# A hybrid decoder block on one core: the end of a gathered tile, its weights, the one-hots of the gates and the layout of the gates

## The chip, the cores and the metric

The kernel runs on one core of a Trainium2 chip. The metric is the time of one execution in device microseconds; the kernel before takes 4811.26 us, the median of three runs from 4801.93 to 4822.15. TensorE multiplies matrices, VectorE, ScalarE and GpSimd work element by element, SyncE only issues transfers, and ScalarE and GpSimd issue transfers too. In the profile they are PE (PEld for the load of its weights), DVE, ACT, POOL and SP; SPq and ACTq are their queues.

## What is computed

A decoder block over 1024 tokens of width 1024: differential attention and a Mamba-2 mixer in parallel, merged, projected and normalised, then a layer of experts (PEER). The change touches only this last layer. Every token picks 8 x 16 = 128 of 16384 experts by its routing scores, and each expert is one row of u and one of v:

```python
top_s, pos = lax.top_k(cand_s, PEER_TOPK)
eidx = jnp.take_along_axis(cand_i, pos, axis=-1)
g = jax.nn.softmax(top_s, axis=-1)
act = jax.nn.gelu(jnp.einsum('thkd,td->thk', expert_u[eidx], tb), approximate=False)
wts = (g * act.astype(jnp.float32)).astype(tb.dtype)
return jnp.einsum('thk,thkd->td', wts, expert_v[eidx])
```

The result, scaled by a gate, is added to 1.19 times the residual x1, and a layer norm (ln2) follows.

## The kernel before

The tokens lie in two halves of four tiles of 128. `run()` (line 1447) first drives the main phase, which is everything up to the routing scores of both halves, and then the dense phase, in the pool `dp`. Each of the two is a generator whose steps have costs. `drive()` emits a step of it and gives the work beside it as much credit as that step cost; `step()` spends the credit on two queues, "side" (gathered tiles) and "urgent" (routing). A scheduler then sets each engine's order by priority, with the main or dense work and everything in `inline()` ahead; each engine runs its own instructions in that order, and GpSimd's is the order of emission. When the dense work is all emitted, what is left of the side work follows.

The experts are worked in two ways.

**Gathered tiles** are tiles 0 and 1 of the first half and 6, 5 and 4 of the second, in this order. `gathered()` (line 1115) loads the tile's hidden rows into gh. Then for each of 128 choices k an indirect transfer on GpSimd (line 1182) brings one row of u for every token into a buffer grow, and VectorE multiplies it with gh and sums it up into act (line 1125). After the gelu, act is transposed into wt. Then 128 transfers bring the rows of v, each for one token, with a row for each of its 128 experts, and TensorE multiplies them with that token's column of weights (line 1290, ps_y). For this the column stands between columns of zeros in a tile own, so that token r's result falls on row r of a group of 16 (OWN) and adds zero to the others. VectorE copies the columns into two own tiles in turn, 2 tokens for each of two halves at a time (line 1152), 32 copies for a tile. The results go through ys into y_d in DRAM. The tile's end follows at once: gy is read back (line 1176), `finish()` (line 1189) loads x1 and three rows of parameters (gr) and does five passes and some small operations on VectorE, and the result is stored. SyncE issues these loads, the next tile's gh and the dense weights in one queue.

**Dense tiles** are 2, 3 and 7: all 16384 experts are computed for them, and the unpicked ones get a gate of zero. `spread()` (line 1228), part of the routing, makes the gates. For each token k a one-hot first_k, scaled by the gates, is made on VectorE (line 1256) and a one-hot second_k on GpSimd (line 1259), 128x128 each, and their product on TensorE (ps_gate) is that token's gate for each of 128x128 experts. Four tokens are copied into a quarter of gs on ScalarE (line 1273), and after eight the single gs buffer is stored into g_d on ScalarE's queue (line 1277). Tiles 2 and 3 are spread during the main phase but for tile 3's last tokens; tile 7 is spread when the dense phase has begun.

`dense()` (line 1292) goes through 128 blocks of 128 experts. Block e's u weights (wraw, split in two parts whi and wlo by ScalarE and VectorE) give ps_u and act_t. Some blocks later, for f = e - lead, act_t is multiplied with the gates gl (line 1322), split into ehi and elo, and multiplied with the weights of v into ps_v. gl holds the gates of eight blocks for three tiles; it is loaded with three transfers when f % 8 == 0 (line 1319), into one of two buffers:

```python
gt = dp.tile([P, len(tiles) * 16, 8, 8], F32, name="gl", tag="gl", bufs=2)
for i, t in enumerate(tiles):
    nc.sync.dma_start(gt[:, i * 16 : i * 16 + 16], self.g_d[t][:, :, f : f + 8, :])
```

g_d is laid out as [expert row, group of 8 tokens, block, token in the group], so a store writes 4 KB in a run and a load reads 8 x 8 numbers, 256 bytes, in a run. Before the first f, `await_gates()` emits routing until tiles 2, 3 and 7 are spread.

Of the kernel before, what the change touches and what calls it, by code (L numbers as in the profile page):

```python
# [47 lines left out]
class Block:  # L48
# [25 lines left out]
    def setup(self):  # L74
# [39 lines left out]

        self.own = []
        for i in range(2):
            self.own.append(cp.tile([P, 4, 31 + OWN], F32, name=f"own{i}"))
            nc.gpsimd.memset(self.own[i], 0.0)

# [14 lines left out]
        self.g_d = {  # L134
            hb * 4 + t: dr.tile([P, 16, P, 8], F32, name=f"g_d{hb * 4 + t}")
            for hb in range(2) for t in range(self.few[hb], 4)
# [977 lines left out]


    def gathered(self, tile_no):
        nc, a, gp = self.nc, self.a, self.gp
# [5 lines left out]
        for k in range(NSEL):  # L1123
            u = self.gather(a["peer_u"], ei, k)
            nc.vector.scalar_tensor_tensor(  # L1125
                u, u, 1.0, h2, op0=ALU.mult, op1=ALU.mult, accum_out=act[:, k : k + 1]
            )
            yield 1.2
        nc.scalar.activation(act, act, AF.Gelu)
# [7 lines left out]

        n = 2 * OWN
        rows = deque()
        for k in range(P + self.rows_by):  # L1140
# [3 lines left out]
            if k >= self.rows_by and k % 2:  # L1144
                j = k - self.rows_by
                b, r = j // n, j % n // 2
                if r == 0:
                    yield from self.claim("side")
                    ps = self.psum("ps_y", tag="gate")
                own = self.own[r // 2 % 2]  # L1150
                if r % 2 == 0:
                    nc.vector.tensor_copy(  # L1152
                        own[:, :, OWN - 1].rearrange("p (h r) -> p h r", h=2),
                        wt[:, b * n : b * n + n].rearrange("p (h r) -> p h r", h=2)[:, :, r : r + 2],
                    )
                for half in range(2):
                    v = rows.popleft()
                    left = own[:, half * 2 + r % 2, OWN - 1 - r : OWN + 31 - r]
                    for c in range(2):
                        at = 32 * (2 * c + half)  # L1160
                        self.inline(
                            nc.tensor.matmul, ps[at : at + 32, :], left, v[:, c * 512 : c * 512 + 512],
                            start=r == 0, stop=r == OWN - 1, skip_group_check=True,
                        )
# [9 lines left out]
            yield 1.2  # L1174
        y = self.row("gy")
        nc.sync.dma_start(y, self.y_d[tile_no])
        self.finish(t0, y)
        del self.picked[tile_no]

    def gather(self, table, ei, k):  # L1180
# [51 lines left out]
    def spread(self, t, fe, g):  # L1232
# [20 lines left out]
        for k in range(P + self.behind_by):  # L1253
            if k < P:
# [3 lines left out]
                )  # L1258
                nc.gpsimd.tensor_scalar(second, self.iota_c, at[:, 1, k : k + 1], None, op0=ALU.is_equal)  # L1259
                ready.append((first, second))  # L1260
            if k >= self.behind_by:
# [14 lines left out]
                if n % 8 == 7:  # L1276
                    nc.scalar.dma_start(self.g_d[t][:, n // 8], gs.rearrange("p t i -> p i t"))
            if k % 2:
# [13 lines left out]
    def dense(self, r):  # L1292
# [7 lines left out]
        for e in range(P + self.lead + 1):  # L1300
# [10 lines left out]
            if f < P:  # L1311
                if f % 8 == 0:
# [5 lines left out]
                    for i, t in enumerate(tiles):  # L1318
                        nc.sync.dma_start(gt[:, i * 16 : i * 16 + 16], self.g_d[t][:, :, f : f + 8, :])
                t = ts.popleft()  # L1320
# [126 lines left out]
    def run(self):  # L1447
# [6 lines left out]
        self.turn, self.dp, self.urgent = 0, None, None  # L1454
        self.claimed, self.spare, self.count = False, iter(()), 0
        with ExitStack() as c:
# [5 lines left out]
            with tc.tile_pool(name="bp", bufs=1) as self.bp, tc.tile_pool(name="mp", bufs=1) as self.mp:  # L1462
                self.drive(self.main(), self.ratio, self.lag[0])
                while self.urgent:
                    self.step()
            with tc.tile_pool(name="dp", bufs=1) as self.dp:
                self.plan(1)
                self.drive(self.dense(self.h2x), self.ratio1, self.lag[1])
                while self.side or self.urgent:
                    self.step()  # L1470


# [71 lines left out]
```

## Time and profile before

| | before |
|---|---|
| median of three runs | 4811.26 us |
| the profiled execution | 4822.5 us, its span 4820.7 us |
| TensorE (PE) busy | 4016.2 us, 83% |
| VectorE (DVE) | 2974.3 us, 62% |
| ScalarE (ACT) | 1423.7 us, 30% |
| GpSimd (POOL) | 1881.6 us, 39% |
| DMA packets | 443648, of them under 512 B 141852 |
| gates stored, line 1277 | 48 transfers of 512 KB |
| gates loaded, line 1319 | 48 transfers of 512 KB |

The profile is that of one execution. Its time is the span and what lies around it. An engine's share is its busy time over the whole span; since the stages of this kernel differ, windows of the trace say more about one of them than the share does. The DMA share of a window is the mean busy share of the 16 DMA engines as it is modelled, and can come out a little over 1.

### The profile page before, as it was taken

To read this page: it belongs to the slowest core of one execution; us is meant where nothing else is said; L and a number is where in the kernel's file an instruction comes from. 1 tells how busy PE (TensorE), PEld (TensorE's weight loads), DVE (VectorE), ACT (ScalarE), POOL (GpSimd) and SP (SyncE) were. 2 spreads that over 40 slices of the span, in tenths; PEclk is the share of its full clock that TensorE was granted. 3 is DMA by queue.
4 is the path that set the end of the run, shared out by engine and by line. 5 is a ranking of instruction groups with operands and counts; after the bars stand their busy time and mean duration, and the time that the engine had idled before them with its cause. 6 is when DMAs were issued, how large, how long until landed. Compare 5 with 4: busy or idle time off the path is not lost.

```text
span 4820.7 us, 52596 instructions
## 1 busy us (share of the span) xinstructions
PE 4016.2 (83%) x17996; PEld 2752.8 (57%) x17996; DVE 2974.3 (62%) x6965; ACT 1423.7 (30%) x2340; POOL 1881.6 (39%) x1720
## 2 busy tenths in 40 slices
PE   6999998998988999988686846867999789999246
PEld 4667667776656755556563325756556676556100
DVE  7664646558999754468872157999322885225940
ACT  3544544324343343432221113322222222222000
POOL 1000000000224744454584546465344565344775
PEclk9999999999898999988897965989999999999679
DMA  7323233443554867778697852998888999888998
GB/s 282 105 70 119 73 107 103 137 147 101 170 163 163 300 232 236 264 266 276 191 303 256 319 195 92 308 311 297 275 280 285 355 333 325 272 284 314 361 393 349
DMA packets 443648, 1134.14 MB, mean 235 GB/s; under 512 B 141852, under 2 KB 164532, under 8 KB 443380
## 3 DMA queue, kind: packets, MB, share of 16 engines
q0 software_dynamic: 191008, 676.42, 39.5%
q1 hardware_dynamic: 218804, 405.04, 26.0%
q10 hardware_dynamic: 33568, 49.32, 2.8%
q8 instruction: 143, 2.34, 0.2%
q14 instruction: 125, 1.02, 0.1%
HBM read 1066.51 MB, written 63.06 MB: 234 GB/s over the span
## 4 chain that ended last, share of the span: by engine, by line
PE 54%; DVE 18%; DMA 13%; issue 8%; POOL 5%; ACT 2%; SPq 1%; DVEq 0%; ACTq 0%; POOLq 0%
PE ps_u L269 9%; PE ps_v L1330 8%; PE ps_y L1290 7%; DVE grow L1125 5%; PE ps_x L269 5%; DMA grow<-in_peer_v,ej 5%; PE ps_b L269 4%; DMA grow<-in_peer_u,ei 3%; PE ps_z L269 3%; PE ps_g L269 2%; POOL grow L1182 2%; DVE wlo L220 2%; POOL second_k L1259 2%; PE ps_vT L269 2%; PE ps_pq L269 2%
## 5 line engine op out<-in xcount | busy, mean ns | idle before, releaser
L1182 POOL DMA_INDIRECT grow<-in_peer_u,ei x640 | 856.0, 1337 | 983.9 <-DVE grow L1125 312.0
L1182 POOL DMA_INDIRECT grow<-in_peer_v,ej x640 | 681.8, 1065 | 731.1 <-PE ps_y L1290 589.0
L219 ACT CAST whi<-wraw 128x1024 fp32r<-128x1024 f32 x498 | 519.9, 1047 | 1390.7 <-PE ps_u L269 548.9
L220 DVE TENSOR_TENSOR wlo<-wraw,whi 128x1024 fp32r<-128x1024 f32 x498 | 607.2, 1220 | 483.5 <-ACT whi L219 431.7
L1125 DVE SCALAR_TENSOR_TENSOR grow<-grow,gh 128x1024 f32<-128x1024 f32 x640 | 771.3, 1220 | 96.9 <-DMA grow<-in_peer_u,ei 95.4
L1290 PE MATMUL ps_y<-grow,own 128*32 128x512 f32 x2560 | 614.6, 636 | 83.7 <-DMA grow<-in_peer_v,ej 63.5
L269 PE MATMUL ps_u<-hhi,whi 128*128 128x384 f32 x1024 | 363.4, 355 | 48.2 <-ACT whi L219 40.8
L269 PE MATMUL ps_u<-hhi,wlo 128*128 128x384 f32 x1024 | 361.7, 353 | 44.2 <-DVE wlo L220 44.0
L1259 POOL TENSOR_SCALAR second_k<-iota_c,at 128x128 f32<-128x128 f32 x384 | 308.6, 814 | 228.3 <-PE ps_gate L1290 181.4
L983 POOL DMA_DIRECT2D h2s_d<-bighi x8 | 4.5, 561 | 915.3 <-ACT bighi L245 915.3
L1152 DVE COPY own<-wt 128x4 f32<-128x4 f32 x160 | 28.6, 182 | 536.5 <-PE ps_y L1290 532.7
L269 PE MATMUL ps_u<-hlo,whi 128*128 128x384 f32 x1024 | 354.9, 347 | 0.0
L1290 PEld LDWEIGHTS ps_y<-grow,own 128*32 128x32 f32 x2560 | 89.9, 111 | 405.7 <-DMA grow<-in_peer_v,ej 203.3
L1290 PE MATMUL ps_gate<-first_k,second_k 128*128 128x128 f32 x768 | 192.7, 386 | 107.7 <-POOL second_k L1259 62.0
L1330 PE MATMUL ps_v<-whi,ehi 128*128 128x512 f32 x768 | 225.2, 411 | 68.0 <-ACT whi L219 49.2
L1330 PE MATMUL ps_v<-wlo,ehi 128*128 128x512 f32 x768 | 256.4, 407 | 23.3 <-DVE wlo L220 23.3
L269 PEld LDWEIGHTS ps_u<-hhi,whi 128*128 128x128 f32 x1024 | 199.8, 195 | 118.2 <-ACT whi L219 52.3
L269 PEld LDWEIGHTS ps_u<-hhi,wlo 128*128 128x128 f32 x1024 | 199.7, 195 | 97.6 <-DVE wlo L220 65.8
L1330 PE MATMUL ps_v<-whi,elo 128*128 128x512 f32 x768 | 249.3, 400 | 0.0
L1290 PEld LDWEIGHTS ps_gate<-first_k,second_k 128*128 128x128 f32 x768 | 152.2, 250 | 157.7 <-POOL second_k L1259 102.4
L1330 PEld LDWEIGHTS ps_v<-whi,ehi 128*128 128x128 f32 x768 | 142.9, 193 | 128.3 <-ACT whi L219 59.9
L269 PEld LDWEIGHTS ps_u<-hlo,whi 128*128 128x128 f32 x1024 | 199.7, 195 | 17.8 <-issue 14.3
(342 smaller groups left out, 8034.9 us busy)
## 6 DMA issues: line engine op xcount, KB each, us to landing
wraw<-in_w_in SPq DMA_DIRECT2D x160, 512.0 KB, 3.7
wraw<-in_peer_uT SPq DMA_DIRECT2D x128, 512.0 KB, 6.3
wraw<-in_peer_v SPq DMA_DIRECT2D x128, 512.0 KB, 6.6
wada<-in_w_adaT SPq DMA_DIRECT2D x48, 512.0 KB, 6.6
g_d<-gs ACTq DMA_DIRECT2D x48, 512.0 KB, 4.3
gl<-g_d SPq DMA_DIRECT2D x48, 512.0 KB, 13.2
cr<-cum_d SPq DMA_DIRECT2D x64, 256.0 KB, 4.2
wraw<-in_w_ssd SPq DMA_DIRECT2D x32, 512.0 KB, 3.7
```

The costliest lines, as they stand in the source:

```text
L219: nc.scalar.copy(hi, raw)
L220: i = nc.vector.tensor_tensor(lo, raw, hi.bitcast(F32), op=ALU.subtract)
L269: i = self.nc.tensor.matmul(ps, w[x][:, k, :], r[y][:, k, :], start=k + n == 0, stop=k == kk - 1 and n == 2)
L983: nc.gpsimd.dma_start(self.h2s_d[part][:, k, :], big[k][part][:, g0:])
L1125: nc.vector.scalar_tensor_tensor(u, u, 1.0, h2, op0=ALU.mult, op1=ALU.mult, accum_out=act[:, k : k + 1])
L1152: nc.vector.tensor_copy(own[:, :, OWN - 1].rearrange("p (h r) -> p h r", h=2), wt[:, b * n : b * n + n].rearrange("p (h r) -> p h r", h=2) ...
L1182: self.nc.gpsimd.indirect_dma_start(out=r, out_offset=None, in_=table, in_offset=bass.IndirectOffsetOnAxis(ap=ei[:, k : k + 1], axis=0),)
L1259: nc.gpsimd.tensor_scalar(second, self.iota_c, at[:, 1, k : k + 1], None, op0=ALU.is_equal)
L1290: return op(*args, **kw)
L1330: nc.tensor.matmul(acc[2 * tt + c], prev[x][:, tt * P : tt * P + P], v[y].rearrange("p k c -> p (k c)")[:, c * 512 : c * 512 + 512], start ...
```

## The change

The change has four parts.

1. The end of a gathered tile (gy, `finish()`) is no longer emitted when its last row of v is, but as `gathered_out()` after row 16 of the next gathered tile's u; the last tile's end comes after everything.
2. In the dense phase the weights are set between zeros eight tokens at a time, in two own tiles of the pool dp with 2 x 8 columns: 8 copies for a tile. Two memsets of 128x752 on GpSimd are new. In the main phase it stays two tokens.
3. In the dense phase second_k is made on VectorE; GpSimd keeps those of tile 2 and of tile 3.
4. g_d is laid out as [expert row, group of 8 blocks, group of 8 tokens, 64]. A store now writes 16 x 128 runs of 256 bytes, and a load reads 128 runs of 4 KB.

```diff
-        self.own = []
-        for i in range(2):
-            self.own.append(cp.tile([P, 4, 31 + OWN], F32, name=f"own{i}"))
-            nc.gpsimd.memset(self.own[i], 0.0)
+        self.own = self.zeros(cp, 2)
...
-            hb * 4 + t: dr.tile([P, 16, P, 8], F32, name=f"g_d{hb * 4 + t}")
+            hb * 4 + t: dr.tile([P, 16, 16, 64], F32, name=f"g_d{hb * 4 + t}")
...
+    def zeros(self, pool, n):
+
+        own = []
+        for i in range(2):
+            own.append(pool.tile([P, 2, n, 31 + OWN], F32, name=f"own{n}_{i}"))
+            self.nc.gpsimd.memset(own[i], 0.0)
+        return own
+
     def gathered(self, tile_no):
...
                 u, u, 1.0, h2, op0=ALU.mult, op1=ALU.mult, accum_out=act[:, k : k + 1]
             )
+            if k == 16:
+                self.gathered_out()
             yield 1.2
...
         n = 2 * OWN
+        owns = self.owns if self.dp else self.own
+        m = owns[0].shape[2]
...
-                own = self.own[r // 2 % 2]
-                if r % 2 == 0:
+                own = owns[r // m % 2]
+                if r % m == 0:
                     nc.vector.tensor_copy(
-                        own[:, :, OWN - 1].rearrange("p (h r) -> p h r", h=2),
-                        wt[:, b * n : b * n + n].rearrange("p (h r) -> p h r", h=2)[:, :, r : r + 2],
+                        own[:, :, :, OWN - 1],
+                        wt[:, b * n : b * n + n].rearrange("p (h r) -> p h r", h=2)[:, :, r : r + m],
                     )
                 for half in range(2):
                     v = rows.popleft()
-                    left = own[:, half * 2 + r % 2, OWN - 1 - r : OWN + 31 - r]
+                    left = own[:, half, r % m, OWN - 1 - r : OWN + 31 - r]
...
-        y = self.row("gy")
-        nc.sync.dma_start(y, self.y_d[tile_no])
-        self.finish(t0, y)
+        self.ended = tile_no
         del self.picked[tile_no]
+
+    def gathered_out(self):
+
+        if self.ended is not None:
+            y = self.row("gy")
+            self.nc.sync.dma_start(y, self.y_d[self.ended])
+            self.finish(self.ended * P, y)
+            self.ended = None
...
-                nc.gpsimd.tensor_scalar(second, self.iota_c, at[:, 1, k : k + 1], None, op0=ALU.is_equal)
+
+                (nc.vector if self.dp else nc.gpsimd).tensor_scalar(
+                    second, self.iota_c, at[:, 1, k : k + 1], None, op0=ALU.is_equal
+                )
...
                 if n % 8 == 7:
-                    nc.scalar.dma_start(self.g_d[t][:, n // 8], gs.rearrange("p t i -> p i t"))
+                    nc.scalar.dma_start(self.g_d[t][:, :, n // 8], gs.rearrange("p t (b i) -> p b (i t)", b=16))
...
                     for i, t in enumerate(tiles):
-                        nc.sync.dma_start(gt[:, i * 16 : i * 16 + 16], self.g_d[t][:, :, f : f + 8, :])
+                        nc.sync.dma_start(
+                            gt[:, i * 16 : i * 16 + 16].rearrange("p g i t -> p g (i t)"), self.g_d[t][:, f // 8]
+                        )
...
             with tc.tile_pool(name="dp", bufs=1) as self.dp:
+                self.owns = self.zeros(self.dp, 8)
                 self.plan(1)
                 self.drive(self.dense(self.h2x), self.ratio1, self.lag[1])
                 while self.side or self.urgent:
                     self.step()
+                self.gathered_out()
```


SyncE's queue at the seam from tile 6 to tile 5, before: wraw are dense weights, gy, gx and gr belong to tile 6's end, gh to tile 5.

```order
L217 DMA wraw<-in_peer_v 128x1024
L217 DMA wraw<-in_peer_uT 128x1024
L1176 DMA gy<-y_d 128x1024
L1192 DMA gx_26168<-x_d 128x1024
L1195 DMA gr_26170<-mod_d 128x1024
L1195 DMA gr_26172<-in_ln_g 128x1024
L1195 DMA gr_26174<-in_ln_b 128x1024
L1121 DMA gh_26213<-h_d 128x1024
L217 DMA wraw<-in_peer_v 128x1024
```

After, the place where gh's load stands now:

```order
L214 DMA wraw<-in_peer_uT 128x1024
L214 DMA wraw<-in_peer_v 128x1024
L1126 DMA gh_26159<-h_d 128x1024
L214 DMA wraw<-in_peer_uT 128x1024
L214 DMA wraw<-in_peer_v 128x1024
```

And the end of tile 6, some twenty rows later:

```order
L214 DMA wraw<-in_peer_uT 128x1024
L1191 DMA gy<-y_d 128x1024
L1207 DMA gx_26372<-x_d 128x1024
L1210 DMA gr_26374<-mod_d 128x1024
L214 DMA wraw<-in_peer_v 128x1024
L1210 DMA gr_26376<-in_ln_g 128x1024
L1210 DMA gr_26378<-in_ln_b 128x1024
```

gh's load has moved ahead of the end's five loads, with dense weights between them.

VectorE at the same seam, before: gy and ln2s belong to tile 6's end, grow to the rows of u of tile 5, the rest to the dense experts (ej, in the second piece, to the routing of tile 4).

```order
L246 TENSOR_TENSOR elo<-act_t,ehi 128x384
L220 TENSOR_TENSOR wlo<-wraw,whi 128x1024
L1197 TENSOR_TENSOR gy<-gy,gr_26170 128x1024
L1202 SCALAR_TENSOR_TENSOR gy<-gx_26168,gy 128x1024
L220 TENSOR_TENSOR wlo<-wraw,whi 128x1024
L1322 TENSOR_TENSOR act_t<-act_t,gl 128x384
L906 BN_STATS ln2s<-gy 128x6 x2
L1125 SCALAR_TENSOR_TENSOR grow,act<-grow,gh_26213 128x1024 x7
L246 TENSOR_TENSOR elo<-act_t,ehi 128x384
```

After:

```order
L243 TENSOR_TENSOR elo<-act_t,ehi 128x384
L217 TENSOR_TENSOR wlo<-wraw,whi 128x1024 x2
L1342 TENSOR_TENSOR act_t<-act_t,gl 128x384
L243 TENSOR_TENSOR elo<-act_t,ehi 128x384
L217 TENSOR_TENSOR wlo<-wraw,whi 128x1024
L1130 SCALAR_TENSOR_TENSOR grow,act<-grow,gh_26159 128x1024 x2
L1239 CAST ej<-ps_ej 128x128
L1130 SCALAR_TENSOR_TENSOR grow,act<-grow,gh_26159 128x1024
L217 TENSOR_TENSOR wlo<-wraw,whi 128x1024
L1342 TENSOR_TENSOR act_t<-act_t,gl 128x384
L243 TENSOR_TENSOR elo<-act_t,ehi 128x384
L1130 SCALAR_TENSOR_TENSOR grow,act<-grow,gh_26159 128x1024
```

The end's rows are gone from here; tile 5's rows of u stand between dense operations.

VectorE in the spreading of tile 7, before, with routing work of the next tile (cand, tkw, val) between the one-hots:

```order
L1256 TENSOR_SCALAR first_k<-iota_c,at 128x128
L1078 TENSOR_TENSOR cand<-val 128x8x4
L1078 TENSOR_TENSOR cand<-val 128x8x3
L1016 MATCH_REPLACE tkw<-val,scr 128x128
L1078 TENSOR_TENSOR cand<-val 128x8x2 x2
L1256 TENSOR_SCALAR first_k<-iota_c,at 128x128
L1016 MATCH_REPLACE tkw<-val,scr 128x128
L1078 TENSOR_TENSOR cand<-val 128x8x2
L1256 TENSOR_SCALAR first_k<-iota_c,at 128x128
L1017 MAX val<-tkw 128x8
```

After:

```order
L1271 TENSOR_SCALAR first_k<-iota_c,at 128x128
L1275 TENSOR_SCALAR second_k<-iota_c,at 128x128
L1015 MAX_INDEX idx<-val,tkw 128x8
L1271 TENSOR_SCALAR first_k<-iota_c,at 128x128
L1275 TENSOR_SCALAR second_k<-iota_c,at 128x128
L1015 MAX_INDEX idx<-val,tkw 128x8
L1271 TENSOR_SCALAR first_k<-iota_c,at 128x128
L1275 TENSOR_SCALAR second_k<-iota_c,at 128x128
L1013 MATCH_REPLACE tkw<-val,scr 128x128
L1271 TENSOR_SCALAR first_k<-iota_c,at 128x128
```

Behind each first_k now stands its second_k, which GpSimd made before.

Two counts of VectorE's order belong to this. Ahead of the multiplication of act_t with gl in block f = 72 stood 391 rows of u and now stand 397, six more of tile 5. Behind the last dense weights (wlo) stood 93 rows of u and now stand 80, all of tile 4.

## Rows read from the trace of the kernel before

**Rows 1.** Windows: length; PE, PEld, DVE, ACT, POOL busy (instructions); clock, DMA share, GB/s
```profile
2815.00:3010.00 195.00, 106.54 (x359) 78.72 (x358) 152.53 (x665) 48.25 (x49) 106.00 (x166) 0.56 0.29 100
2900.00:2992.00 92.00, 77.36 (x256) 59.38 (x256) 76.12 (x350) 31.59 (x30) 82.00 (x128) 0.57 0.22 86
3045.00:3350.00 305.00, 228.26 (x1012) 193.32 (x1011) 289.82 (x768) 75.04 (x101) 181.78 (x127) 0.91 0.93 320
3350.00:3706.00 356.00, 338.67 (x1567) 205.23 (x1567) 122.43 (x185) 78.23 (x109) 146.33 (x129) 1.00 0.84 281
3706.00:4018.00 312.00, 265.63 (x1257) 227.71 (x1256) 246.41 (x381) 87.24 (x120) 190.00 (x129) 0.94 0.96 337
4018.00:4372.00 354.00, 345.45 (x1586) 207.91 (x1584) 100.31 (x149) 79.27 (x111) 145.75 (x129) 0.99 0.83 286
4372.00:4530.00 158.00, 108.24 (x468) 84.45 (x464) 124.08 (x210) 32.18 (x44) 90.22 (x67) 0.86 0.92 339
4530.00:4626.00 96.00, 0.00 (x0) 0.00 (x0) 87.62 (x160) 0.00 (x0) 71.97 (x64) 0.50 0.98 369
```

**Rows 2.** The chain of waits, 3700 to 4030 us: start us, us, what
```profile
3843.21 13.50 DMA wraw<-in_peer_uT
...
3936.42 10.83 DMA wraw<-in_peer_v
...
4016.84 12.53 DMA wraw<-in_peer_v
```

**Rows 3.** Windows inside u5 and at the start of u4, as in rows 1
```profile
3706.00:3750.00 44.00, 43.55 (x211) 32.86 (x210) 19.93 (x24) 14.57 (x21) 9.09 (x8) 1.00 0.79 279
3835.00:3860.00 25.00, 11.75 (x54) 9.88 (x54) 12.51 (x19) 4.60 (x6) 8.57 (x7) 0.77 0.98 309
3860.00:3920.00 60.00, 56.53 (x279) 50.52 (x278) 56.47 (x88) 18.52 (x26) 46.75 (x29) 0.98 0.95 348
3920.00:3950.00 30.00, 17.18 (x84) 15.30 (x83) 16.18 (x26) 6.47 (x9) 13.47 (x11) 0.84 1.03 338
4000.00:4030.00 30.00, 20.65 (x105) 18.17 (x103) 21.21 (x34) 6.29 (x10) 20.20 (x14) 0.93 1.07 349
4372.00:4417.00 45.00, 44.56 (x217) 35.01 (x214) 20.01 (x27) 12.97 (x19) 8.84 (x8) 1.00 0.82 296
```

**Rows 4.** SyncE's timeline at a burst and at a seam: start us, us, issue
```profile
3831.84 11.27 SPq L1319 DMA_DIRECT2D gl<-g_d  x3
...
4398.81 0.33 SPq L1176 DMA_DIRECT2D gy<-y_d  x1
...
4403.48 0.44 SPq L1121 DMA_DIRECT2D gh<-h_d  x1
```

**Rows 5.** GpSimd's timeline at the start of tile 4's rows; idle time before in brackets
```profile
4417.34 1.68 POOL L1182 DMA_INDIRECT grow<-in_peer_u,ei  x1 [28.24 <-DVE grow L1125]
```

**Rows 6.** Three windows of u6 around loads of gl, 74 us, summed
```profile
sum 74.00, PE 48.65 PEld 40.85 DVE 66.75 ACT 11.31 POOL 41.16; mean PE 16.22 PEld 13.62 DVE 22.25 ACT 3.77 POOL 13.72
```

**Rows 7.** One pass of an end on VectorE: ns min/median/max, first and last start
```profile
L1204 DVE SCALAR_TENSOR_TENSOR gy<-gy,ln2g,gr x5: 1268/1271/1276, 2113.7 to 4812.5; 128x1024 f32<-128x1024 f32 x5
```

**Rows 8.** Groups by line, 2900 to 2992 us: count, busy us, mean ns, idle before
```profile
L1256 DVE TENSOR_SCALAR first_k<-iota_c,at 128x128 f32<-128x128 f32 x128 | 44.8, 355 | 14.5 <-PE ps_gate L1290 12.8 <-ACT at L1249 1.4
...
L1259 POOL TENSOR_SCALAR second_k<-iota_c,at 128x128 f32<-128x128 f32 x128 | 82.0, 658 | 41.3 <-ACT at L1249 33.4 <-PE ps_gate L1290 7.9
...
L1273 ACT COPY gs<-ps_gate 128x512 f32<-128x512 f32 x30 | 31.6, 1104 | 57.9 <-PE ps_gate L1290 35.0 <-DMA g_d<-gs 22.9
```

**Rows 9.** From issue to landing, line 1277 (g_d<-gs), then line 1319 (gl<-g_d)
```profile
DMA to landing us min/median/max: 2.6/4.3/9.8
...
DMA to landing us min/median/max: 4.8/13.2/21.0
```

**Rows 10.** The copies of weights, 2740 to 2830 us, and what VectorE waited for
```profile
L1152 DVE COPY own<-wt x12: 171/172/284, 2740.2 to 2808.9; 128x4 f32<-128x4 f32 x12
...
  PE ps_y L1290: 62.7, 12
```

More of the change, by code (lines that the diff above doesn't have):

```diff
@@ L1454, in run @@
         self.turn, self.dp, self.urgent = 0, None, None
-        self.claimed, self.spare, self.count = False, iter(()), 0
+        self.claimed, self.spare, self.count, self.ended = False, iter(()), 0, None
         with ExitStack() as c:
```

## The prediction

> **What bounds the kernel now.** I began with busy time by stage [rows 1], because one share for the whole span mixes stages with different limits. Nearly all that the change touches lies from 2815 us on. I name the stages there by what GpSimd gathers beside the dense experts: u6 (3045 to 3350 us, rows of u for tile 6), v6 (3350 to 3706), u5 (3706 to 4018), v5 (4018 to 4372), u4 (4372 to 4626, in which the dense part ends at about 4530); ahead of them stands the spreading of tile 7 (2815 to 3010). The reader is to see that they have different bounds. In v6 and v5 TensorE is busy for 338.67 of 356 and 345.45 of 354 us: nothing on VectorE or in a queue is worth more there than the 17.3 and 8.6 us that are left. In u6 VectorE is the bound, 289.82 of 305. In u5 neither is: TensorE 265.63 and VectorE 246.41 of 312, with the DMA engines at 0.96. In the spreading GpSimd is, 82.00 of 92 us.
>
> Then I asked what ends last in u5. The chain [rows 2] names three loads of dense weights, 13.50, 10.83 and 12.53 us, 36.9 together. The windows around them [rows 3] show both engines falling there (TensorE 11.75, 17.18 and 20.65 of 25, 30 and 30 us; VectorE 12.51, 16.18, 21.21), while between them TensorE has 56.53 and VectorE 56.47 of 60. SyncE's queue [rows 4] gives the reason: at 3831.84 three loads of gl take it 11.27 us to issue, and the weights that TensorE wants next stand behind them. A load of gl in runs of 256 B lands after 13.2 us in the median, the store of g_d, of the same size in runs of 4 KB, after 4.3 [rows 9].
>
> The last thing read is the seam between two gathered tiles. From 3706 to 3750 and from 4372 to 4417 VectorE is busy for 19.93 of 44 and 20.01 of 45 us, with the DMA engines at 0.79 and 0.82 [rows 3]. GpSimd waits 28.24 us at the second for VectorE to free a row [rows 5], since the new tile's rows need gh, and gh's load stands on SyncE behind gy's [rows 4], which waits for the stores of y_d.
>
> **The change part by part.** *Gates in 4 KB runs, load side.* What is lost in u5's three bursts is VectorE's idle time there, 12.5 + 13.8 + 8.8 = 35 us, which agrees with the 36.9 of the chain. Three loads of 512 KB still have to come: 1.57 MB at the 348 GB/s of the window between the bursts is 4.5 us each, so 35 - 13.5 = 22 would be gained by the queue. *The end moved into the next tile's rows.* In the order gh's load goes up some twenty rows, away from gy's, and the first rows of u stand with nothing of gy ahead of them; six rows more of tile 5 stand ahead of the same dense block, 6 x 1.5 us (64 rows in 96 us, 4530 to 4626 [rows 1]) = 9 us. Both together would be 31 in u5. They meet the same limit, the DMA engines: those are idle for 0.04 x 312 = 12.5 us, and what the runs of 256 B cost them is read from the rate at full share, 309/0.98 = 315, 338/1.03 = 328 and 349/1.07 = 326 GB/s in the bursts against 348/0.95 = 366 between: 14%, 10% and 11% of 24.5, 31 and 32 us, 10 us in all. So u5 gives at most 22.5 if the engines never rest; I take 22, as the two sums of 22 and 31 both reach this bound, and 10 to 32 for the range.
>
> In u4 the order has 13 more rows of u ahead of the last weights, so that 13 fewer are left when the dense part ends: 13 x 1.5 = 19.5 us of the stretch 4530 to 4626. They must be loaded earlier, where the DMA engines have 0.08 x 158 = 12.6 us to spare. I take 13, range 5 to 20. GpSimd's 28 us wait is the same time seen from there and isn't counted again.
>
> In v6 and v5 the bursts and the waits for zeroed weights share 26 us of idle TensorE; I take a quarter, 6, range 0 to 14, because TensorE is what is late next. In u6 the bursts leave VectorE 74 - 66.75 = 7.3 us idle [rows 6]; a little over half, 4, may go. But the end of tile 1 now falls into u6: five passes of about 1.27 us [rows 7], 6.4 us on an engine that is 95% busy. So u6 loses 2 (range: gains 5 to loses 10).
>
> *Late one-hots on VectorE, and the store.* GpSimd's 128 second_k at 658 ns are 82 us beside 128 first_k at 355 ns on VectorE [rows 8]. The move takes the bound off GpSimd and puts 128 operations on VectorE, which has 92 - 76.12 = 15.9 us to spare there [rows 1]. No row shows second_k on VectorE. Bounds are the 172 ns of a copy of four columns [rows 10] and the 355 ns of first_k, the same tile with one operand more; I take 300, near the latter: 38 us, less 15.9, is +22.5. Against it stand the end of tile 1, which leaves this stretch (-6.4), and the first load of gl, which the dense part waits for (13.2 to about 5 us, -8). *Weights eight tokens at a time*: VectorE waits for TensorE 62.7 us in the last 70 us of tile 1's weights [rows 10], and the routing queued behind them now passes sooner; since the first first_k behind them wait for GpSimd anyway, I take -3. The sum is +5. With second_k at either bound the stage comes to -18 (and ten for the weights) or to +31 (nothing fits into the idle time).
>
> *The store's form.* It goes from 16 runs to 16 x 128 runs of 256 B. One gs buffer is filled by two copies, stored, and waited for: copies of 1104 ns and a landing of 4.3 now. A single load in 256 B runs lands at best in 4.8 [rows 9], when the queue is empty, as it is here with the DMA engines at 0.22. Two copies and 4.8 are 7.0 us for eight tokens; VectorE would need (92 + 22)/16 = 7.1. I cost the store at nothing because VectorE hides it, barely; the first rival prices what it costs if that cover is gone.
>
> The Trainium skill speaks against this half of the change: "DMA: Bandwidth & Descriptors", Specifications, gives 512 B as the least transfer for line rate and says that below it the engine does a read-modify-write. The rows agree with it on loads only (13.2 against 4.3 us); no row here shows a store in runs of 256 B. By that rule the store takes over the price that the load loses, and the first rival would be the forecast.
>
> In the main phase the end of tile 0 moves into tile 1's rows, beside matmuls that set the end; 0, within 8 either way. The tail from 4626 us keeps its rows, and the end of tile 4 still stands last: 0.
>
> **Sum:** -22 - 13 - 6 + 2 + 5 = -34 us. The profiled execution took 4822.5 us (span 4820.7), 11 over the median of 4811.3. Taken off the median: 4777 us.
>
> **The rivals.** *A, the store of 256 B runs becomes the bound of tile 7's spreading.* For it: one gs buffer, no cover beyond 7.1 us for eight tokens. Against it: idle DMA engines. It begins at a landing of 7.1 - 2.2 = 4.9 us, eats the whole gain at (114 + 34)/16 - 2.2 = 7.1, and makes the kernel slower by over 0.5% at 8.6. At 13.2, the landing of the loads, the loop is 16 x 15.4 = 246 us, 132 over the 114 that I count: 4909 us. *B, u5 is bound by bytes, not by their form.* For it: the DMA engines are at 0.98 to 1.07 in the bursts, and the gathers ask for whatever is freed. Then u5's 22 are lost, and -12 are left: 4799 us, no change by what can be told here. *C, the queue is all.* If SyncE's issue alone made the bursts, u5 gives 32, u4 20, v6 and v5 14, u6 5 and the spreading 10: -81, 4730 us.
>
> **How the numbers follow.** 0.5% (24 us) is about what a measurement of this kernel can tell from no change: below 4787 counts as faster, above 4835 as slower. Forecast 0.54 (4745 to 4795), B 0.26, A 0.12, C 0.08. Faster: C 0.08, of the forecast 0.50, of B 0.03, 0.61. Slower: of A 0.10, 0.01 of B: 0.11. Same: the rest, 0.28. The forecast's own low end is 22 - 32, 13 - 20 and the others at their better bounds, about -75; C ends lower still, and half of it is left out: 4732. At the other end the range takes in B with the spreading at +31 and leaves out A beyond a landing of about 7.8: 4822.
>
> **What would show it right or wrong.** In u5 no chain piece on a weight load above 5 us, TensorE over 85% in each burst, the gl loads issued in under 1 us each and landing near 5: else B. At the seams VectorE goes from wlo straight to rows of u, and GpSimd's wait of 28 us is gone. In the spreading VectorE is over 95% busy, GpSimd idle, and ScalarE's copies wait for VectorE's one-hots; if they wait for g_d instead, with landings over 7 us, it is A. After the last weights some 80 rows of u are left rather than 93. What would upset the sum most is a slower store, or second_k far from 300 ns.

## The result

The changed kernel takes 4752.81 us, the median of four runs from 4745.85 to 4761.72, against 4815.27 for the kernel before beside it: a ratio of 0.9875, 95% interval 0.9846 to 0.9903, 62 us less. Its profiled execution has a span of 4752.9 us against 4820.7, 67.8 us less. The page of the changed kernel:

```profile
span 4752.9 us, 52286 instructions
...
PE 4001.6 (84%) x17996; PEld 2740.8 (58%) x17996; DVE 2979.8 (63%) x7021; ACT 1423.7 (30%) x2340; POOL 1815.0 (38%) x1594
```

The engines do nearly the same work, with tile 7's second_k moved from GpSimd (1815.0 us for 1881.6) to VectorE; what went is idle time. The stages of [rows 1] in the changed kernel, with the same columns (its u6 begins at 3046, v6 at 3337, u5 at 3682, v5 at 3957, u4 at 4311, and the window of its dense part is cut at 4460, 18 us behind the last product of ps_v):

```profile
2815.00:3010.00 195.00, 112.19 (x371) 77.10 (x371) 160.00 (x770) 46.31 (x46) 29.82 (x41) 0.58 0.38 95
3046.00:3337.00 291.00, 228.22 (x1021) 190.83 (x1021) 287.01 (x694) 73.43 (x100) 176.41 (x128) 0.94 0.94 345
3337.00:3682.00 345.00, 341.25 (x1604) 211.07 (x1604) 134.43 (x260) 82.70 (x116) 147.96 (x128) 1.00 0.83 296
3682.00:3957.00 275.00, 248.97 (x1161) 211.83 (x1160) 238.07 (x372) 79.68 (x109) 192.10 (x129) 0.96 0.98 374
3957.00:4311.00 354.00, 350.89 (x1616) 212.22 (x1615) 100.89 (x129) 81.33 (x113) 146.10 (x128) 1.00 0.81 286
4311.00:4460.00 149.00, 114.63 (x498) 88.84 (x496) 123.10 (x206) 34.82 (x47) 89.88 (x69) 0.92 0.96 355
4460.00:4555.00 95.00, 0.00 (x0) 0.00 (x0) 87.48 (x162) 0.00 (x0) 69.42 (x61) 0.50 0.99 378
```

The reader is to see u5: 275 us for 312, with the DMA engines at 374 GB/s for 337, and TensorE at 91% for 85. In v6 TensorE's idle time is down from 17.3 to 3.8 us. In u6 VectorE has 4 us left of 15, and its operations are fewer, 694 for 768.

Taken from GpSimd's first gather of one stage to that of the next, in one profiled execution each, the stages of the kernel before, the changed one and four of the experiments are, in us:

| | before | changed | gates alone | all but the gates | end at once | loads twice |
|---|---|---|---|---|---|---|
| to u6 | 3043.4 | 3046.2 | 3051.9 | 3053.6 | 3060.2 | 3047.8 |
| u6 | 307.9 | 290.9 | 284.8 | 317.0 | 286.8 | 299.6 |
| v6 | 356.4 | 345.5 | 335.0 | 357.0 | 342.8 | 348.9 |
| u5 | 310.9 | 274.3 | 289.4 | 293.8 | 293.2 | 271.7 |
| v5 | 354.3 | 354.6 | 354.5 | 357.2 | 344.9 | 357.7 |
| u4 | 252.4 | 244.0 | 251.4 | 242.2 | 249.9 | 240.0 |
| v4 and the end | 195.5 | 197.5 | 213.7 | 214.6 | 214.3 | 198.1 |

The last row goes by when a kernel was measured and not by the kernel: the three that were measured together take 214 us for this DMA-bound tail, the others 195 to 198, and the changed kernel took 213.2 in its second measurement, where it has 197.5 here. What differs between them no run here shows. So medians are compared by their ratio to the kernel before that was measured beside them. Ahead of the tail the second measurement of the changed kernel has 3037.3, 291.3, 344.6, 274.5, 354.6 and 244.1 us: the stages from u6 to u4 can be compared between columns, the first row only to about 9 us.

The three waits for dense weights that the chain of u5 had [rows 2] are gone. The one long DMA piece that the chain of the changed kernel has there is a gather (start us, us):

```profile
3814.94 12.98 DMA grow<-in_peer_u,ei
```

The issue of gl's loads in u5 (line 1337: count and ns, min/median/max) and their landing:

```profile
L1337 SPq DMA_DIRECT2D gl<-g_d x9: 326/443/551, 3718.8 to 3882.2; - x9
...
DMA to landing us min/median/max: 8.5/12.4/17.8
```

A load holds SyncE for 0.44 us, where three took 11.27 [rows 4]. It lands after 12.4 us, where the loads of u5 took 17.3 in the kernel before (the 13.2 of [rows 9] are those of all its stages); that is not near the 5 us that the prediction gave as a sign, yet nothing in u5 waits for it. What ScalarE waits for before it splits dense weights (engine, line, what it waited for: us, times, longest), between 3050 and 4430 us, in the kernel before:

```profile
ACT whi L219 <- DMA wraw<-in_peer_uT: 33.5, 8, 11.8
ACT whi L219 <- DMA wraw<-in_peer_v: 31.0, 10, 11.2
```

And in the changed kernel:

```profile
ACT whi L216 <- DMA wraw<-in_peer_uT: 12.2, 4, 9.1
...
ACT whi L216 <- DMA wraw<-in_peer_v: 9.0, 4, 5.2
```

64.5 us of late weights have become 21.2.

### The profile page after: what moved, and what is told of

Same layout as the page of the kernel before. It is cut to its first block, busy times and chain, and to the rows that moved or that the text cites. A ratio compares the mean times of both kernels' runs of the same rounds, so it can differ in the third digit from the quotient of the medians.

```text
span 4752.9 us, 52286 instructions
## 1 busy us (share of the span) xinstructions
PE 4001.6 (84%) x17996; PEld 2740.8 (58%) x17996; DVE 2979.8 (63%) x7021; ACT 1423.7 (30%) x2340; POOL 1815.0 (38%) x1594
## 4 chain that ended last, share of the span: by engine, by line
PE 57%; DVE 19%; DMA 11%; issue 6%; POOL 4%; ACT 2%; SPq 0%; ACTq 0%; POOLq 0%; DVEq 0%
PE ps_u L266 10%; PE ps_v L1350 9%; PE ps_y L1308 8%; DVE grow L1130 5%; DMA grow<-in_peer_v,ej 5%; PE ps_x L266 5%; PE ps_b L266 4%; PE ps_z L266 3%; DMA grow<-in_peer_u,ei 3%; PE ps_pq L266 3%; POOL grow L1197 2%; DVE wlo L217 2%; PE ps_g L266 2%; PE ps_vT L266 2%; PE ps_s L433 2%
## 5 line engine op out<-in xcount | busy, mean ns | idle before, releaser
L1275 POOL TENSOR_SCALAR second_k<-iota_c,at 128x128 f32<-128x128 f32 x256 | 231.1, 910 | 168.1 <-PE ps_gate L1308 152.5
L266 PEld LDWEIGHTS ps_u<-hhi,wlo 128*128 128x128 f32 x1024 | 199.6, 195 | 110.1 <-DVE wlo L217 75.4
L1161 DVE COPY own<-wt 128x4 f32<-128x4 f32 (+1 forms) x88 | 16.4, 191 | 373.6 <-PE ps_y L1308 367.2
```

The lines of the kernel that those rows point to most:

```text
L266: i = self.nc.tensor.matmul(ps, w[x][:, k, :], r[y][:, k, :], start=k + n == 0, stop=k == kk - 1 and n == 2)
L1161: nc.vector.tensor_copy(own[:, :, :, OWN - 1], wt[:, b * n : b * n + n].rearrange("p (h r) -> p h r", h=2)[:, :, r : r + m],)
L1275: (nc.vector if self.dp else nc.gpsimd).tensor_scalar(second, self.iota_c, at[:, 1, k : k + 1], None, op0=ALU.is_equal)
```

## The experiments

**Which part gave it.** Theory Q puts most of it on the loads of gl, rival E on the seams between tiles. The first kernel is the one before with the new layout alone:

```diff
-            hb * 4 + t: dr.tile([P, 16, P, 8], F32, name=f"g_d{hb * 4 + t}")
+            hb * 4 + t: dr.tile([P, 16, 16, 64], F32, name=f"g_d{hb * 4 + t}")
...
-                    nc.scalar.dma_start(self.g_d[t][:, n // 8], gs.rearrange("p t i -> p i t"))
+                    nc.scalar.dma_start(self.g_d[t][:, :, n // 8], gs.rearrange("p t (b i) -> p b (i t)", b=16))
...
-                        nc.sync.dma_start(gt[:, i * 16 : i * 16 + 16], self.g_d[t][:, :, f : f + 8, :])
+                        nc.sync.dma_start(
+                            gt[:, i * 16 : i * 16 + 16].rearrange("p g i t -> p g (i t)"), self.g_d[t][:, f // 8]
+                        )
```

> The kernel before with the new layout of g_d alone (stores in runs of 256 B, loads of gl in runs of 4 KB). Theory Q, the loads of gl held SyncE's queue and the DMA engines in the bursts, and that is most of the 62 us: 35 to 50 us faster than before, u5 25 us or more shorter, no chain piece of over 5 us on a dense weight load in u5. Rival E, the seams between gathered tiles are most of it: 10 to 20 us faster, u5 at most 12 us shorter.

It takes 4786.08 us, ratio 0.9895 (0.9870 to 0.9921), 51 us by the ratio; its chain in u5 has no wait for dense weights. u6 is 23, v6 21 and u5 21.5 us shorter than in the kernel before; Q had asked for 25 or more in u5.

The second undoes these three places in the changed kernel:

> The changed kernel with the old layout of g_d (loads of gl in runs of 256 B). Theory Q: 12 to 27 us faster than before, and the three waits for weights in u5 are back at 10 us and more. Rival E: 40 to 50 us faster.

4832.32 us, ratio 0.9984 (0.9972 to 0.9995): 8 us are left, below the 12 that Q gave as the least. Its chain in u5 waits for dense weights again, for 10.2, 9.4 and 11.7 us. So by the time of the whole kernel nearly all comes from the layout, more than Q had put. By stage it is less one-sided: without the layout u5 is still 17.1 us shorter and u4 10.2, and u6 is 9.1 us longer.

The third emits the end at once:

```diff
-            if k == 16:
-                self.gathered_out()
...
         self.ended = tile_no
+        self.gathered_out()
```

> The changed kernel with a gathered tile's end emitted at once again. Theory Q: 45 to 55 us faster than before, 10 to 17 us lost, half in u5 and half in u4, where GpSimd waits 25 us at each seam again. Rival E: 20 to 30 us faster only.

4791.98 us, ratio 0.9903 (0.9879 to 0.9927); the changed kernel has 0.9875 and, in its second measurement, 0.9855. So the moved end is worth 0.3 to 0.5%, 13 to 23 us, a little more than Q's 10 to 17 at the upper end and far from E; the interval overlaps with that of the first measurement (0.9846 to 0.9903) and just misses that of the second (0.9833 to 0.9876). GpSimd's waits at the two seams are back, where its longest in the changed kernel are 5.9 and 5.3 us. Its timeline at the first (idle time ahead of the operation in brackets):

```profile
3735.16 1.68 POOL L1196 DMA_INDIRECT grow<-in_peer_u,ei  x1 [26.63 <-DVE grow L1130]
```

And at the second:

```profile
4369.96 1.01 POOL L1196 DMA_INDIRECT grow<-in_peer_u,ei  x1 [24.96 <-DVE grow L1130]
```

u5 is 19 and u4 6 us longer than in the changed kernel, v5 10 shorter.

**Two tokens, and the one-hots.** These two undo one part each:

```diff
-        owns = self.owns if self.dp else self.own
+        owns = self.own
...
-                self.owns = self.zeros(self.dp, 8)
```

> The changed kernel with two tokens for a copy of weights in the dense phase too. Theory: VectorE's waits for TensorE in v6 and v5 cover nothing that is late, within 6 us of the changed kernel. Rival: they hold back the split of dense weights, and v6 and v5 are 10 us longer together.

```diff
-    (nc.vector if self.dp else nc.gpsimd).tensor_scalar(
+    nc.gpsimd.tensor_scalar(
```

> The changed kernel with second_k on GpSimd throughout. By the sum of the prediction (22.5 us of VectorE's time more, nothing else late) it is up to 15 us faster than the changed kernel. If GpSimd's 82 us was the bound and VectorE had room, it is 5 to 15 us slower than the changed kernel, all of it between tile 1's last rows and the first row of u6.

Two tokens: 4747.24 us, ratio 0.9851 (0.9825 to 0.9877), v6 343.7 and v5 351.2 us: the rival's 10 us are not there. One-hots on GpSimd: 4742.6 us, ratio 0.9837 (0.9810 to 0.9863), its span 4754.4 and its first use of gl at 3004.2 us, where the changed kernel has 4752.9 and 3005.0. Neither part can be told from nothing, if anything the kernel is faster without it. By the ratios the kernel with one-hots on GpSimd is 9 to 18 us faster than the changed one, which the first expectation allows, but its trace does not show that in the stage that the expectation was about: there was no bound on GpSimd to take away, nor did VectorE's 128 operations cost anything there.

**Why a burst cost what it did.** Gates alone gained 51 us where the prediction had 22 for u5 and some 10 for the other stages. The price may be DMA time, which runs of 256 B take more of, or the queue. To put DMA time alone back, the next kernel copies what each load of gl brings a second time, in 4 KB runs, to a place that nothing reads:

```diff
...
+                        if f:
+                            nc.sync.dma_start(self.twice[i], self.g_d[t][:, f // 8])
```

> The changed kernel; each load of gl but the first three is followed by a copy of the same bytes in runs of 4 KB from g_d to a spare place in DRAM that nothing reads. It holds SyncE's queue for 0.4 us more per load, but adds about the DMA time that the runs of 256 B had cost before (a burst of three 512 KB loads 8 instead of 4 us of all sixteen engines). If DMA time is the price of a burst, wherever it falls: 40 to 60 us slower than the changed kernel, back near the kernel before. If the long issue on SyncE, with dense weights queued behind it, was the price: at most 15 us slower than the changed kernel.

4770.86 us, ratio 0.9900 (0.9875 to 0.9925): 0.25 and 0.45% over the two measurements of the changed kernel, 12 to 22 us, and 11 in the span. But the copies do not stand where the loads do:

```profile
L1342 SPq DMA_DIRECT2D twice<-g_d x45: 469/470/1087, 2233.9 to 3092.9; - x45
```

No load depends on its copy, and all 45 went out as soon as a tile's gates lay in DRAM, the last at 3093 us, ahead of the first burst of the dense part behind the spreading (3131 us). So this run does not show what DMA time costs in a burst. The packets of the trace give its size: in u5 of the kernel before 22116 packets of 256 B took 29.0 us of the sixteen DMA engines; at 180 ns for a packet of 4 KB, as in the kernel with gates alone, the same bytes would take 15.5, an estimate from these two. Of the 21.5 us that gates alone gave in u5 some 13 may thus be DMA time, and no run here parts them from the queue.

What the queue did can be read from the traces. From 3111 us on three loads of gl held SyncE for 12.0 us a burst, in the changed kernel for 1.4. In eleven of these twelve bursts the first dense weights behind the loads were issued 0.1 us after them, and their own issue took 3.7 to 8.7 us, for 0.33 elsewhere; no issue of dense weights takes over 1 us in the changed kernel. Once issued, the weights behind a burst landed after 8.1 to 14.3 us in the kernel before and 10.2 to 13.3 in the changed one, where the trace has it: what went is the time ahead of their issue.

Then the other way: the kernel before, its runs of 256 B left as they are, but taken apart. First in six pieces, a group of eight blocks ahead, one to each step of a block:

```diff
...
+                q = f % 8 - 1
+                if 0 <= q < 6 and f // 8 * 8 + 8 < P:
+                    f1, t, g0 = f // 8 * 8 + 8, tiles[q // 2], q % 2 * 8
+                    nc.sync.dma_start(
+                        nx[:, q * 8 : q * 8 + 8], self.g_d[t][:, g0 : g0 + 8, f1 : f1 + 8, :]
+                    )
```

> The kernel before, with gl loaded in runs of 256 B as before, but a group of eight blocks ahead and in six pieces, one behind each of the blocks' steps, so that SyncE's queue is never held by 6144 runs at once; the bytes and their form stay. If the held queue is the cost of the bursts: within 12 us of the kernel with the new layout alone. If the form is (what 256 B runs take from the DMA engines): at most 12 us faster than before, since the same 10 us for three bursts are only spread out.

4842.37 us, ratio 1.001 (0.9993 to 1.0027): nothing gained. By the expectation that spoke for the form and against the held queue, but the trace shows why the kernel doesn't tell them apart. The issue of gl from 3050 us on, in the kernel before:

```profile
L1319 SPq DMA_DIRECT2D gl<-g_d x36: 523/4838/10169, 3111.3 to 4228.2; - x36
```

In this one, and below it a group of pieces in SyncE's order:

```profile
L1326 SPq DMA_DIRECT2D gl<-g_d x72: 377/2272/7297, 3109.3 to 4229.5; - x72
...
3832.40 17.91 SPq L1326 DMA_DIRECT2D gl<-g_d  x6
```

The scheduler put the pieces together again: in seven of the twelve groups all six stand in a row, in the other five in two rows of three and three or four and two. Summed up, SyncE is held for 170 us by the pieces, and was for 144 by the whole loads (for 17 in the changed kernel). What I had meant to take away was still there.

So the pieces were moved to ScalarE's queue, nothing else changed:

```diff
-                    nc.sync.dma_start(
+                    nc.scalar.dma_start(
                         nx[:, q * 8 : q * 8 + 8], self.g_d[t][:, g0 : g0 + 8, f1 : f1 + 8, :]
                     )
```

> The kernel before with gl in pieces as in the experiment on pieces, runs of 256 B, but issued from ScalarE's queue in place of SyncE's. If what the runs of 256 B cost is that dense weights stand behind them in SyncE's queue: 25 to 50 us faster than before, less what ScalarE loses by issuing. If it is the runs themselves, wherever they stand: within 10 us of the kernel before.

4915.55 us, ratio 1.0162 (1.0141 to 1.0183), 78 us slower, which neither side had. The trace says more about the cause. The issue of gl on ScalarE, 3050 to 4500 us:

```profile
L1326 ACTq DMA_DIRECT2D gl<-g_d x72: 366/2294/11608, 3104.4 to 4304.9; - x72
```

What ScalarE waited for there (two rows of its waits):

```profile
ACT whi L219 <- issue: 90.8, 8, 19.7
ACT ehi L245 <- issue: 48.6, 7, 14.6
```

And TensorE (its three longest):

```profile
PE ps_u L269 <- DVE wlo L220: 55.6, 26, 8.2
PE ps_v L1339 <- ACT whi L219: 49.8, 23, 15.4
PE ps_u L269 <- ACT act_t L1305: 49.7, 11, 12.6
```

The wait for dense weights has all but gone from ScalarE (0.5 us for 64.5), and 139 us of "issue" have come: the engine stands for 190 us in all to send off 72 pieces. On SyncE no issue of dense weights takes over 1 us now, though the same runs of 256 B go through the same DMA engines. New for TensorE is the wait for act_t, 2.8 us in the kernel before; its waits for whi come to 75.4 us, for 86.7 there, with ScalarE's issue behind them in place of late weights. A load in 256 B runs thus has a price that goes with the queue it stands in, the time that its issue holds what the issuing engine has behind it: dense weights on SyncE, the split of dense weights and the gelu on ScalarE. What I underrated is that ScalarE has more to lose than SyncE. How much of the price in u5 is the queue and how much DMA time stays open.

**What sets the spreading of tile 7.** In the changed kernel ScalarE's timeline of the spreading (start, us, operation, in brackets what it waited for):

```profile
2970.41 2.02 ACT L1291 COPY gs<-ps_gate 128x512 f32<-128x512 f32 x2 [4.16 <-DMA g_d<-gs]
2972.46 0.52 ACTq L1295 DMA_DIRECT2D g_d<-gs  x1
2976.58 2.01 ACT L1291 COPY gs<-ps_gate 128x512 f32<-128x512 f32 x2 [4.15 <-DMA g_d<-gs]
2978.62 0.52 ACTq L1295 DMA_DIRECT2D g_d<-gs  x1
```

Every 6.2 us eight tokens, two copies and the landing of the store: the single gs is the bound, and would be with second_k on either engine (stores 6.1 to 6.2 us apart there as well). gs was doubled, with second_k left on VectorE, and in a second kernel every other second_k was put on GpSimd besides; the third has both, and two tokens for a copy of weights:

```diff
-    gs = gp.tile([P, D], F32, name="gs", tag="gs", bufs=1).rearrange("p (i t) -> p t i", t=8)
+    gs = (self.row("gs") if self.dp else gp.tile([P, D], F32, name="gs", tag="gs", bufs=1)).rearrange("p (i t) -> p t i", t=8)
...
-    (nc.vector if self.dp else nc.gpsimd).tensor_scalar(
+    (nc.vector if self.dp and k % 2 else nc.gpsimd).tensor_scalar(
```

> The changed kernel with gs doubled (taken from the ring of row buffers in the dense phase) and second_k still on VectorE. In the trace of the changed kernel the spreading of tile 7 stores every 6.2 us, two copies and a landing of 4.06, with second_k on VectorE and on GpSimd alike. If the store is the bound: the period falls to what VectorE needs, about 5 us, and the first use of gl comes 12 to 20 us earlier. If VectorE is: the period stays over 6.

> The changed kernel with two parts of the spreading of tile 7 altered: every other second_k on GpSimd, and gs taken from the ring of row buffers, so that it is double. If VectorE's one-hots and the wait of the single gs for its store (6.1 us for eight tokens in the trace of the changed kernel) set the spreading's end: 10 to 25 us faster than the changed kernel, all ahead of u6. If something else is late there (the routing ahead of the one-hots, TensorE at half clock): within 5 us.

> The changed kernel with every other second_k on GpSimd, a double gs, and two tokens for a copy of weights throughout. 30 to 50 us faster than the changed kernel: 41 us as with the eight tokens, and up to 10 more if the copies of eight tokens hold TensorE up in the last rows of tile 1 (2818.7 us against 2826.2 for its last product).

> The changed kernel itself, beside the three others, so that what they are compared with is from the same chip. 50 to 70 us faster than before.

Measured beside each other, the changed kernel takes 4764.27 us (ratio 0.9855, 0.9833 to 0.9876), that with gs doubled 4747.95 (0.9826, 0.9806 to 0.9845), and with all three 4737.67 (0.9789, 0.9770 to 0.9808). With the one-hots shared out and eight tokens, measured at another time, it is 4717.87 (0.9786, 0.9759 to 0.9813). So the last two are alike by ratio, and the one measured beside the changed kernel beats it by 27 us, where 30 to 50 were expected; by ratio the other is 33 to 43 us faster than the changed kernel, for an expected 10 to 25. The two tokens add nothing that can be told. With gs doubled alone the stores are 3.6 us apart, with the one-hots shared 3.2, and the first use of gl comes at 2952.8 and 2955.3 us, where the changed kernel has 3005.0 and 2996.1 in its two profiles: 40 to 52 us earlier where 12 to 20 were expected. What VectorE needs is 3.6 us and not the 5 of the expectation: with gs doubled alone a token's two one-hots follow the last two every 0.45 us, since their records of 0.34 and 0.28 us overlap, and eight times 0.45 is the pace of the stores. ScalarE now goes from one gate to the next, its two copies and an issue (the kernel with shared one-hots):

```profile
2928.54 0.52 ACTq L1295 DMA_DIRECT2D g_d<-gs  x1
2929.16 1.09 ACT L1291 COPY gs<-ps_gate 128x512 f32<-128x512 f32 x1 [0.65 <-PE ps_gate L1308]
2930.60 1.09 ACT L1291 COPY gs<-ps_gate 128x512 f32<-128x512 f32 x1 [0.35 <-PE ps_gate L1308]
2931.72 0.52 ACTq L1295 DMA_DIRECT2D g_d<-gs  x1
```

Not all of it reaches the end. GpSimd's first gather of u6 moves up by only 10 to 20 us, to 3027 us (3046 and 3037 in the changed kernel), as tile 6's routing on VectorE is late next (waits of GpSimd, 2950 to 3030 us, same kernel):

```profile
POOL grow L1197 <- DVE idx L1012: 81.7, 1, 81.7
```

## Why the prediction was right, and where its terms were not

The time is 24 us below the 4777 that were predicted and inside the range, faster as forecast; the layout of the gates, named first, gives nearly all of it, and SyncE's queue, held by loads of gl, was its way at least in part. That the time fell into the range is in part luck: u6 gave 17 us for a reason that the prediction did not have. Term by term, by the profiled executions (-67.8 in all where -34 was summed up; -34 is also short of the 62 of the medians):

- **u5, -22 predicted, -36.6 measured.** The loads of gl gave 22 and the rows 9; I cut the 31 to 22 by a bound from the DMA engines, reckoned from their busy share and the GB/s in and between bursts. That step failed: the changed kernel moves 374 GB/s at a share of 0.98 where I took 366 as the most, so a share near 1 did not mean that nothing more would go through. The term of the loads had the right size, 21.5 us with gates alone. The rows of the moved end were mis-sized: 15 to 19 us where I had 9 (15.1 between gates alone and the changed kernel, 17.1 with all but the gates, 18.9 with the end at once).
- **u6, +2 predicted, -17.0 measured.** I took VectorE's idle time in three bursts, 7.3 us, as all there was to gain. Its idle time in the whole stage fell from 15.2 to 4.0 us. The larger part I had not seen at all: the emission is the same, but the scheduler's order is not. Between the first and the last row of u of tile 6 VectorE has 299 operations of routing in the order of the kernel before and 228 in the changed one, the rest behind them, where it isn't the bound. In the trace the routing takes VectorE 63.4 us there for 81.9, from each start to the next and waits left out, against 6.7 us that tile 1's end brought in. The new layout alone does it (224), and without it the order has 297; why, no run here shows. So part of what the layout gave is neither queue nor DMA time. The order was there to be counted before.
- **v6 and v5, -6 predicted, -10.6 measured** (-10.9 and +0.3). The 17.3 us of TensorE's idle time in v6 went nearly whole, and v5 gained nothing. Within the range of 0 to 14.
- **u4, -13 predicted, -8.4 measured.** The last product of ps_v ends at about 4492 us in the kernel before and not at the 4530 that I took as the end of the dense part. Cut there, u4 falls into these two windows, first in the kernel before, then in the changed one:

```profile
4372.81:4492.30 119.49, 107.07 (x463) 83.97 (x461) 88.00 (x139) 31.69 (x43) 63.53 (x45) 0.96 0.89 328
4492.30:4625.18 132.88, 0.36 (x2) 0.00 (x0) 122.10 (x227) 0.00 (x0) 97.33 (x84) 0.52 0.99 372
...
4311.41:4441.70 130.29, 113.84 (x495) 88.43 (x494) 104.98 (x167) 34.82 (x47) 76.13 (x57) 0.96 0.96 357
4441.70:4555.40 113.70, 0.38 (x2) 0.00 (x0) 106.00 (x200) 0.00 (x0) 83.17 (x71) 0.52 0.98 372
```

  The stretch behind the dense part is 19.2 us shorter, as the 13 rows at 1.5 us had it (19.5), and the dense part, which now takes these rows in, is 10.8 us longer, where I let 6.5 be lost.
- **The spreading, +5 predicted, +2.8 measured**, with all that lies ahead of it (in the second measurement of the changed kernel it is -6.1, so the size is not told from nothing). The reasons were not right. A second_k on VectorE lasts 293 ns, where I took 300:

```profile
L1271 DVE TENSOR_SCALAR first_k<-iota_c,at 128x128 f32<-128x128 f32 x119 | 41.5, 349 | 0.0
L1275 DVE TENSOR_SCALAR second_k<-iota_c,at 128x128 f32<-128x128 f32 x119 | 34.9, 293 | 0.0
```

  But it overlaps with its neighbours and adds only 0.20 us from start to start, 26 us for 128 and not 38, and it is hidden, while the store is not. From the keys of tile 7 to its last store the kernel before takes 96.4 us (2897.8 to 2994.2) and the changed one 110.4 (2886.6 to 2997.0), +14, with a landing of 4.0 us in the spreading for 2.6. That is rival A's mechanism, at a price of 14 and not 132 us, as the store lands below the low bound that was taken from a load (4.8). By A's own condition it would not have begun under a landing of 4.9; what failed is the cover of 7.1 us for eight tokens, which VectorE was said to give and of which its one-hots need 3.6. It was masked: the stage begins 11.2 us earlier, where -9.4 was taken for tile 1's end and the weights. The -8 for the first load of gl did not come; from the last store to the first use it is 7.9 us in both.

The rule of the Trainium skill on runs under 512 B ("DMA: Bandwidth & Descriptors", Specifications) is borne out in kind, on both sides: a store of 512 KB in 256 B runs lands 1.4 us later than one in 4 KB runs. That the store would take over the price that the load loses, as the prediction read the rule, did not come: the loop of the store costs 14 us, and the load's price was in part its issue.

Rival B, that u5 is bound by bytes whatever their form, fell with u5 of gates alone, 21.5 us shorter at 362 GB/s for 337 (columns as in rows 1):

```profile
3671.75:3961.10 289.35, 258.26 (x1228) 221.64 (x1227) 243.61 (x378) 84.31 (x116) 185.25 (x128) 0.96 0.95 362
```

Rival C, that the queue is all, came nearest in the sum, 81 us for 67.8, but not by its parts: it had 20 for u4, 5 for u6 and 10 for the spreading, and -8.4, -17.0 and +2.8 were measured.

## What to carry to other kernels

Look at how long a transfer holds the engine that issues it, and at what stands behind it in that queue, before its bytes: a few thousand short runs among loads that an engine waits for can hold these up by 12 us a burst, and cutting the loads in pieces that are then issued in a row, or moving them to a busier engine, gave nothing back. See in the trace where a scheduler has put what an experiment adds, before reading its time. When a part is moved to another engine, ask what the loop waits for with the part gone: here one buffer of 4 KB set the pace on either engine. And count the operations of an order before and after on the engine that bounds a stage, since a scheduler may move work that the edit doesn't name.

## What the runs showed of the hardware

The time that the issue of a load holds its engine does not go by the count of its runs alone. In the kernel before, from 3111 us on, the first of three loads of 2048 runs of 256 B is issued in 0.52 us in each of the twelve bursts, as is a store of 2048 such runs on ScalarE in the spreading of the changed kernel; the second and third take 3.4 to 10.2 us. Dense weights in 128 runs of 4 KB, 0.33 us elsewhere, take 3.7 to 8.7 right behind them. So the wait goes with the queue that the short runs were put into: with the loads on ScalarE no weights on SyncE take over 1 us. How fast such a queue empties no run here shows. A packet of 256 B took 20.6 ns of a DMA engine in these loads, one of 4 KB 180.

TensorE's granted clock in the spreading was at its lower level where the gate products wait for the store (and in the kernel before, with 119 products in the same 50 us), and near the upper where they follow each other. The changed kernel, 2900 to 2950 us (columns as in rows 1):

```profile
2900.00:2950.00 50.00, 45.29 (x131) 32.61 (x131) 50.00 (x300) 14.63 (x15) 0.00 (x0) 0.50 0.39 82
```

That with gs doubled and the one-hots shared:

```profile
2900.00:2950.00 50.00, 46.45 (x235) 34.67 (x233) 49.93 (x200) 32.72 (x30) 35.68 (x58) 0.98 0.82 184
```

0.50 is 1.2 GHz and 0.98 nearly all of the stretch at 2.4. In the first the products wait for the store through the single gs, 131 of them in 50 us, in the second there are 235. Part of what the first use of gl moved up may be this, but no run here parts it from the rest.
